# The first norm of a two-layer trunk, fed tile by tile of x, with three pairs of weight column tiles in flight

## The chip, the cores and the metric

The kernel runs as one program on one NeuronCore of one Trainium2 chip. The metric is the device time in microseconds of one execution; lower is better. Before the change it is 1466.57 us (median of 3 runs, 1466.33 to 1467.88).

The engines are named as the profile names them: PE is TensorE (matmuls; PEld its weight loads), DVE is VectorE, ACT is ScalarE, POOL is GpSimd, and SP is SyncE, whose queue issues nearly all loads here. Each engine works through its own queue in order; an instruction whose input is missing holds up everything behind it on that engine.

## The reference, cut to what matters

Two layers of a diffusion backbone over 384 tokens of width 1024: 128 context tokens and 256 latent ones, each group with its own conditioning vector. Each layer is FFN, mixer, FFN, and each of the three is modulated by nine vectors per layer:

```
mod = silu(cond) @ w_mod[l] + b_mod[l]                 # (1024) @ (1024, 9216), one cond per group
sh1, sc1, g1, sh2, sc2, g2, sh3, sc3, g3 = split(mod, 9)
x = x + 0.5*g1 * swiglu(modulate(rmsnorm(x, norm_g[l,0]), sh1, sc1), w1, w3, w2)
x = x + g2 * mixer(modulate(rmsnorm(x, norm_g[l,1]), sh2, sc2))
x = x + 0.5*g3 * swiglu(modulate(rmsnorm(x, norm_g[l,2]), sh3, sc3), ...)
rmsnorm(x, g)  = x * rsqrt(mean(x*x) + eps) * g ;  modulate(x, sh, sc) = x*(1+sc) + sh
swiglu(x, ...) = (silu(x @ w1) * (x @ w3)) @ w2        # 1024 -> 2816 -> 1024, all float32
```

Before the first matmul of the first FFN can run, the kernel needs sh1 and sc1 of layer 0 (8 MB of w_mod), x (1.5 MB) and the first weights.

## The kernel before, in words

Everything is transposed: x lies in SBUF as 8 K tiles of 128 rows (features) by 384 columns (tokens). All weights are 128x128 tiles, packed on the host in the order in which the program reads them, 16 tiles to a 1 MB chunk (156 chunks). Every float32 product is made of three float32r matmuls: each weight and each activation is split into a high part (a rounded copy, `hi`) and a low part (the rest, `lo`), and `mm3` (line 436) issues hi*hi, hi*lo, lo*hi. So one weight tile is three matmuls of 384 or 386 columns, and one chunk is 48. `w_split` (391) makes `hi` of half a chunk (8 tiles) by a copy on ACT or DVE, and `w_lo` (410) makes `lo` on DVE; when both halves are split, the chunk's buffer is free and `w_load` (381) asks SP for another one. There are 3 chunk buffers (`rawp`, line 261).

In the first FFN the norm is not applied to x ahead of the matmul. `prep` (522) scales a tile of x by A = norm_g*(1+sc1), a column per token group, and appends the shift sh1 as two extra columns (386 columns); the factor rsqrt(mean(x*x)) is a number per token and is multiplied in when PSUM is read (`up_evac`, 649). `rstd_chain` (546) gets that factor from the sum of squares that `prep` collects, by one matmul with a matrix of 1/1024. `normed_all` (560) meanwhile makes the fully normed x on the idle DVE; from some column tile on the FFN uses it instead.

`ffn` (602) loops over 22 column tiles f; each has a w1 and a w3 column of 8 K tiles, 16 weight tiles, 48 matmuls. For f = 0 the last K tile comes last for both; otherwise the whole w1 column is made and then the w3 column. Each f has a pair of PSUM banks (tag `sc`, two pairs).

The start is written out by hand. The 8 MB of w_mod for sc1 (k = 1) and then sh1 (k = 0) come in eight 1 MB tiles, four per vector: rows of K, 1024 columns. For each, 8 matmuls with silu(cond) as weights (32 columns wide, four of them side by side in the array) add to one PSUM tile; the result is two rows of 1024, which two transposes turn into columns. Only after all four tiles of sc1 are added does A exist, and `prep` runs for all eight tiles of x; only after all four of sh1 do the two shift columns exist. The loads stand on SP's queue in this order: four tiles for sc1, the eight tiles of x, four for sh1, three weight chunks, and then what is needed later (c as rows, two tiles of w_mod for DVE, tables).

All other modulation vectors (128 tiles of 0.5 MB) are made on DVE by `mod_one` (476), when it has nothing else to do; the program's own rough clock (`Clock`, `Sched`) decides while the program is written where such side work is put between the matmuls. It orders the instructions and nothing else.

Of the kernel before, what the change touches and what calls it, by code (L numbers as in the profile page):

```python
# [19 lines left out]
P = 128  # L20
NP_, NS = 128, 256
T = NP_ + NS
TB = T + 2
# [7 lines left out]
N_SLAB = 79  # L31
# [16 lines left out]
class Event:  # L48
    """Something that a chain of instructions has still to emit, with the tiles that it leaves."""
# [5 lines left out]
class Banks:  # L55
    """PSUM tiles of one tag: how many may be in use at a time, and when the free ones fell free."""
# [5 lines left out]
class Idle:  # L62
    """Ready when an engine has nothing else queued."""
# [19 lines left out]
class Clock:  # L83
    """Rough times of the engines while the program is written: they order the emission and nothing else."""
# [34 lines left out]
class Sched:  # L119
    """Emits the stages of side chains between pieces of the matmul stream, each when its inputs should be there."""  # L120
# [81 lines left out]
class Eng:  # L202
    """An engine's instructions, timed by the clock as they are written."""
# [50 lines left out]
def emit(tc, D, order):  # L254
    nc = tc.nc
    ctx = ExitStack()
    with ctx:
# [3 lines left out]
        rawp = pool("raw", 3)  # L261
# [60 lines left out]
        def copy(out, in_, scale=None):  # L322
            """out = in_ (times a column), on the engine that should be done with it first."""
            k = {} if scale is None else {"scale": scale}
            r = max(clock.at(in_)[0], clock.at(out)[0])
            ta = max(clock.free["ACT"], r) + S_.cost("activation", out, [in_], k)
            td = max(clock.free["DVE"], r) + V.cost("tensor_copy", out, [in_] if scale is None else [in_, scale], k)
            if td + ON_ACT < ta:
                if scale is None:
                    V.tensor_copy(out, in_)  # L330
                else:
                    V.tensor_scalar(out, in_, scale, None, ALU.mult)
            else:
                act(out, in_, AF.Copy, **k)

# [36 lines left out]
        class WS:  # L372
            raw, hi, lo, rest = {}, {}, {}, {}
            asked, due = set(), []
            loaded = split = n = 0
# [5 lines left out]
        def w_load():  # L381
            c = WS.loaded
# [93 lines left out]
        def mod_one():  # L476
            """Generator: one modulation tile, a condition per stage."""
# [17 lines left out]
        mod_on = Event()  # L495

        def mod_all():
# [16 lines left out]
        class XS:  # L514
            hi, lo, ev, sq, A, sh = [], [], [], None, None, None
# [6 lines left out]
        def prep(d, with_sh=True):  # L522
            """Generator: scaled x as two float32r parts, and the sum of squares."""
            q = sl()
            hi = XS.hi[d] = sl(F32R, TB)
            lo = XS.lo[d] = sl(F32R, TB)
            act(q, x[d], AF.Square)
# [4 lines left out]
            yield hi, q  # L532
            if XS.sq is None:
                XS.sq = q
            else:
                V.tensor_tensor(XS.sq, XS.sq, q, ALU.add)
# [4 lines left out]
            sched.fire(XS.ev[d], hi, lo, XS.sq)  # L541
# [4 lines left out]
        def rstd_chain():  # L546
# [11 lines left out]
            sched.add(gen(RS.t, RS.ev, XS.ev))  # L558
# [43 lines left out]
        def ffn(l, n, nxt):  # L602
# [6 lines left out]
            for f in range(FF):  # L609
# [24 lines left out]
                sched.add(up_evac(ps, hs[f]))  # L634
# [14 lines left out]
        def up_evac(ps, h):  # L649
            yield ps  # L650
            bc = small.tile([P, 2, 2], F32, tag="bc2", name=nm("bc"))
            V.tensor_copy(bc, ps[:, :, T:TB])
            t, u = sl(), sl()
            V.tensor_tensor(t, ps[:, 0, :T], RS.t, ALU.mult)
            V.tensor_tensor(u, ps[:, 1, :T], RS.t, ALU.mult)
            free(scb, ps, u)
# [57 lines left out]
        def qk_norm(t, bc, gate, gs):  # L714
            """Generator: leaves the normed rows in t, then returns the two parts of the rotated ones."""
# [107 lines left out]
        def transposed(src, n):  # L823
            """w (128 queries, n*128 keys) -> SBUF (keys, n, queries)."""
# [22 lines left out]
        def proj_pass(tiles, key, done, low):  # L847
            """Projection tiles in order; the first two share a K order that leaves the last tile of x late."""
# [32 lines left out]
        def out_pass(key, gm, nxt, ready, free_at, early, wide):  # L881
            """Output projection. The K tiles in `early` come first: x takes their part while the others are computed."""
# [8 lines left out]
            def slot(t, ps):  # L891
                """A bank that has nothing to do: kept while there are units to come."""
# [351 lines left out]
        def wm_load(i):  # L1244
            t = rawp.tile([P, 2, 1024], F32, tag="raw", name=nm("wm0"))
            nc.sync.dma_start(t, D["wm0"][i])
            landed(t, 1 << 20, sched.now())
            return t

        def mixer_consts():  # L1250
            yield RS.ev, el, pp
            # differential lambda, negated
# [5 lines left out]
            # -8 * softplus(-lam) on (128, 2 directions, 4 tiles); log1p by its series in z / (2 + z)  # L1258
# [24 lines left out]
        wm0 = [wm_load(i) for i in range(3)]  # L1283
        for k in (1, 0):
            ps = mmt()
            for i in range(4):
                w = wm0.pop(0)
                for s in range(2):
                    for g in range(4):
                        TE.matmul(ps[32 * g:32 * g + 32, 0:256], lhsT=scT[:, 2 * i + s, :],  # L1290
                                  rhs=w[:, s, 256 * g:256 * (g + 1)], start=i + s == 0, stop=i + s == 4)
                j = (4 if k == 0 else 0) + i + 3
                if j < 8:
                    if j == 4:
                        for d in range(KD):
                            nc.sync.dma_start(x[d], D["xT"][d])  # L1296
                    wm0.append(wm_load(j))
                else:
                    w_load()
                    if j == 10:  # L1300
                        nc.sync.dma_start(cbc, D["c_rows"].partition_broadcast(P))
                        landed(cbc, 1 << 20)
                        mod_load(nc.sync)
                        mod_load(nc.sync)
                        nc.sync.dma_start(cst, D["cst"])
                        nc.sync.dma_start(el, D["e_lam"].partition_broadcast(P))
                        landed(el, 1 << 19)
            mrow = sl()
            V.tensor_copy(mrow[:, 0:256], ps[:, 0:256])
            free(mmb, ps, mrow)  # L1310
            pt = mst()
            for b in range(2):
                TE.transpose(pt[:, b * P:(b + 1) * P], mrow[:, b * P:(b + 1) * P], ident)
            M[0, k] = cpool.tile([P, 8, 2], F32, name=f"M0_{k}")
            pv = pt[:, 0:256].rearrange("p (c g r) -> p g c r", c=2, g=4)
            V.tensor_copy(M[0, k].rearrange("p (g c) j -> p g c j", g=4), pv[:, :, :, 0:2])
            free(msb, pt, M[0, k])
            mod_finish(0, k)
            mod_done.add((0, k))
            if k == 1:  # L1320
                prep_begin(0, 0)
                for d in range(KD):
                    for _ in prep(d, False):
                        pass
        sched.add(mod_all(), 2)
        sched.fire(mod_on)
        RS.ev = Event()
        XS.sh = M[0, 0]
        w_split()
        for d in range(KD):  # L1330
            act(XS.hi[d][:, T:TB], XS.sh[:, d, :], AF.Copy)
        w_lo(0, WS.rest[0])
        for d in range(KD):
            V.tensor_tensor(XS.lo[d][:, T:TB], XS.sh[:, d, :], r32(XS.hi[d][:, T:TB]), ALU.subtract)
# [6 lines left out]
        ffn(0, 0, (0, 1))  # L1341
# [8 lines left out]
# order of the 64 rows of a q or k head on the partitions: the two rows of a rotary pair side by side  # L1350
# [136 lines left out]
```

## Time and profile before

| | |
|---|---|
| median of 3 runs | 1466.57 us |
| span of the profiled execution | 1464.2 us |
| PE busy | 1436.7 us, 98% |
| DVE busy | 1115.4 us, 76% |
| ACT busy | 659.8 us, 45% |
| DMA, mean over the span | 171 GB/s, 250.67 MB |

The profiled execution's own time is its span of 1464.2 us and what lies around the span; the median of the runs is 2.4 us above the span. In the 40 slices of the page the PE row is `4999999999999999999999999999999999999998`: of the whole program only the first slice (36.6 us) is not full. The row that names the engine of the chain that ended last says PE 95%, DMA 2%, DVE 2%.

How to read it: an engine's share is a mean over stages. What a change at the start is worth must be read from the start itself: when the first column tiles are done, and which of loads, DVE and PE is the last to be ready for them.

### The profile page before, as it was taken

To read this page: it belongs to the slowest core of one execution; us is meant where nothing else is said; L and a number is where in the kernel's file an instruction comes from. 1 tells how busy PE (TensorE), PEld (TensorE's weight loads), DVE (VectorE), ACT (ScalarE), POOL (GpSimd) and SP (SyncE) were. 2 spreads that over 40 slices of the span, in tenths; PEclk is the share of its full clock that TensorE was granted. 3 is DMA by queue.
4 is the path that set the end of the run, shared out by engine and by line. 5 is a ranking of instruction groups with operands and counts; after the bars stand their busy time and mean duration, and the time that the engine had idled before them with its cause. 6 is when DMAs were issued, how large, how long until landed. Compare 5 with 4: busy or idle time off the path is not lost.

```text
span 1464.2 us, 21823 instructions
## 1 busy us (share of the span) xinstructions
PE 1436.7 (98%) x8354; PEld 1398.4 (96%) x8354; DVE 1115.4 (76%) x2103; ACT 659.8 (45%) x1193; POOL 103.8 (7%) x214
## 2 busy tenths in 40 slices
PE   4999999999999999999999999999999999999998
PEld 1999999998889999999999999999998899999998
DVE  3899999969998998999979997444698795444332
ACT  3643333348875633333345333333477664333321
POOL 0001111110220011111100110000100000000000
PEclk9999999999999999999999999999999999999999
DMA  9557767652322366766744766333331233333430
GB/s 361 216 185 257 246 245 257 235 173 101 120 99 97 140 230 236 254 243 231 254 177 153 251 243 196 135 119 130 117 107 51 77 120 115 133 126 116 146 135 22
DMA packets 49560, 250.67 MB, mean 171 GB/s; under 512 B 6464, under 2 KB 10960, under 8 KB 28336
## 3 DMA queue, kind: packets, MB, share of 16 engines
q1 hardware_dynamic: 29664, 180.05, 34.0%
q0 software_dynamic: 19792, 69.23, 14.2%
q8 instruction: 66, 1.08, 0.3%
q14 instruction: 38, 0.31, 0.1%
HBM read 244.53 MB, written 2.36 MB: 169 GB/s over the span
## 4 chain that ended last, share of the span: by engine, by line
PE 95%; DMA 2%; DVE 2%; ACT 1%; issue 0%; SPq 0%; DVEq 0%; ACTq 0%
PE sc L214 54%; PE mm L214 36%; PE ms L214 5%; DVE s L214 1%; DMA wm<-in_wm 1%; DMA s<-in_xT 1%; DMA raw<-in_wst 0%; DVE lo L214 0%; ACT s L214 0%; DMA s<-s 0%; ACT hi L214 0%; ACT L317 0%; SPq L737 0%; SPq L1296 0%; DVEq L1434 0%
## 5 line engine op out<-in xcount | busy, mean ns | idle before, releaser
L214 PE MATMUL sc<-s,hi 128*128 128x384 f32 (+1 forms) x2816 | 726.3, 339 | 2.3 <-ACT s L214 1.4
L214 ACT ACTIVATE hi<-raw 128x1024 fp32r<-128x1024 f32 x298 | 315.7, 1060 | 541.7 <-PE sc L214 307.4
L214 DVE TENSOR_TENSOR lo<-raw,hi 128x1024 fp32r<-128x1024 f32 x312 | 381.3, 1223 | 231.2 <-ACT hi L214 230.0
L214 PE MATMUL mm<-s,hi 128*128 128x384 f32 (+1 forms) x2072 | 545.8, 344 | 2.3 <-DVE s L214 2.3
L214 PEld LDWEIGHTS sc<-s,hi 128*128 128x128 f32 x2816 | 512.6, 188 | 5.0 <-ACT s L214 1.8
L214 PE MATMUL sc<-s,lo 128*128 128x384 f32 (+1 forms) x1408 | 475.4, 338 | 0.0
L214 PEld LDWEIGHTS mm<-s,hi 128*128 128x128 f32 x2072 | 372.9, 188 | 12.4 <-issue 3.0
L214 PE MATMUL mm<-s,lo 128*128 128x384 f32 (+1 forms) x1036 | 349.1, 337 | 0.0
L214 DVE CUSTOM_DVE_ANT_0 junk<-wm,cbc 128x1024 bf16<-128x1024 f32 x256 | 312.6, 1221 | 11.0 <-DMA wm<-in_wmt 8.3
L214 PEld LDWEIGHTS sc<-s,lo 128*128 128x128 f32 x1408 | 265.0, 188 | 0.0
L214 PEld LDWEIGHTS mm<-s,lo 128*128 128x128 f32 x1036 | 194.7, 188 | 0.0
L214 ACT ACTIVATE s<-s 128x384 f32<-128x384 f32 (+3 forms) x215 | 108.0, 507 | 171.9 <-DVE s L214 157.0
L214 DVE TENSOR_TENSOR s<-s,s 128x384 fp32r<-128x384 f32 (+6 forms) x214 | 112.0, 528 | 20.0 <-ACT s L214 18.9
L214 POOL DMA_DIRECT2D wm<-in_wmt x126 | 66.6, 528 | 695.1 <-DVE M L214 674.2
L214 DVE SCALAR_TENSOR_TENSOR s<-s,M,s 128x128 fp32r<-128x128 f32 (+3 forms) x256 | 92.4, 416 | 3.8 <-ACT s L214 3.7
L214 ACT ACTIVATE s<-s,M 128x256 fp32r<-128x256 f32 (+1 forms) x167 | 66.3, 446 | 11.0 <-DVE s L214 8.1
L214 DVE SCALAR_TENSOR_TENSOR s<-mm,M,s 128x128 f32<-128x128 f32 x104 | 38.5, 412 | 32.2 <-PE mm L214 32.2
L214 DVE TENSOR_TENSOR s<-sc,s 128x384 f32<-128x384 f32 x106 | 56.8, 551 | 0.0
L214 PE MATMUL sc<-s,s 128*128 128x384 f32 (+2 forms) x208 | 49.0, 373 | 0.7 <-ACT s L214 0.7
L214 ACT ACTIVATE s<-ms 128x384 f32<-128x384 f32 (+3 forms) x80 | 31.8, 423 | 29.8 <-PE ms L214 29.5
L214 PEld LDWEIGHTS sc<-s,s 128*128 128x128 f32 x208 | 34.1, 189 | 7.0 <-ACT s L214 1.3
L214 ACT ACTIVATE s<-sc,sm 128x385 f32<-128x385 f32 (+3 forms) x72 | 35.9, 511 | 0.0
(107 smaller groups left out, 635.1 us busy)
## 6 DMA issues: line engine op xcount, KB each, us to landing
raw<-in_wst SPq DMA_DIRECT2D x156, 1024.0 KB, 5.0
wm<-in_wmt POOLq DMA_DIRECT2D x126, 512.0 KB, 3.8
wm<-in_wm SPq DMA_DIRECT2D x8, 1024.0 KB, 7.6
s<-s SPq DMA_DIRECT2D x36, 64.0 KB, 2.4
s<-in_xT SPq DMA_DIRECT2D x8, 192.0 KB, 7.4
out_y<-s SPq DMA_DIRECT2D x8, 192.0 KB, 1.9
cbc<-in_c_rows SPq DMA_DIRECT2D x1, 1024.0 KB, 8.4
wm<-in_wmt SPq DMA_DIRECT2D x2, 512.0 KB, 9.7
```

The lines of the kernel that those rows point to most:

```text
L214: r = fn(*a, **k)
```

## The change

- The eight w_mod tiles are cut the other way. `wm0[d]` holds columns d*128 to d*128+127 of sc1 and of sh1 with all of their 1024 rows, 8 KB per partition in one row. One 1 MB load gives A and sh1 of x's tile d alone. Per tile `first_mod` issues 8 matmuls as before, copies the PSUM rows to SBUF on DVE, and turns them into columns by two matmuls with a 128x2 selector (`sel`), which also adds up the four parts; two DVE instructions read PSUM and leave A and sh1 of this tile, and `prep` of this tile follows.
- The eight loads use six buffers: `cbc` (0, 4), the two halves of `modp` (1, 5), and chunk buffers (2, 3, 6, 7), of which there are now 4 (before 3). The slab of 384-column tiles has 74 (before 79).
- On SP's queue the tiles of x and the first weight chunks stand between them.
- The squares of x are summed by a chain of their own (`first_sq`), as x lands.
- The first FFN starts with `lead=3`: three column tiles f = 0, 1, 2 share the K loop. For each K tile of x all six columns (w1, w3 of three f) get their three matmuls, 18 in all; f = 2 uses the two `mm` banks.
- DVE's modulation tiles, their silu and the constants of the mixer wait for `calm`, which is fired at f = 5; the first 48 modulation tiles then no longer stop during the mixer.
- `up_evac` copies the two shift columns with two instructions, since the two banks may be apart.
- While the first tiles are loaded, `w_next` splits weights ahead only once their chunk has landed.

The diff, cut to its core:

```diff
-N_SLAB = 79
+N_SLAB = 74
...
-        rawp = pool("raw", 3)
+        rawp = pool("raw", 4)
...
             while WS.split <= min(g + 3, 2 * N_CHUNK - 1):
+                if WS.split > g and (WS.split // 2 not in WS.raw and WS.first or WS.split // 2 in WS.raw
+                                     and clock.at(WS.raw[WS.split // 2])[0] > sched.now() + 0.5):
+                    break
                 w_split()
...
         def mod_all():
-            yield cbc, RS.ev
+            yield cbc, calm
             act(cbc, cbc, AF.Silu)
             while mod_at[0] < len(mod_todo):
-                yield mod_on
+                if mod_at[0] >= 48:
+                    yield mod_on
                 yield from mod_one()
...
-            for f in range(FF):
+            if lead:
+                up = []
...
+                for k in range(8):
+                    sched.wait(XS.ev[k])
+                    for f in range(lead):
+                        for m in range(2):
+                            mm3(up[f][m][:, :TB], ("w1" if m == 0 else "w3", l, n, k, f), XS.hi[k], XS.lo[k], k == 0, k == 7)
+                        if k == 7:
+                            sched.wait(RS.ev)
+                            hs.append([None, None, Event()])
+                            sched.add(up_evac(*up[f], hs[f]))
+            for f in range(lead, FF):
+                if f == lead + 2:
+                    sched.fire(calm)
...
+        def first_mod(d):
+            w = m0.pop(d)
+            yield tuple(w) + (msb,)
+            ps = mst()
+            for i in range(2):
+                for g in range(4):
+                    j = 2 * g + i
+                    TE.matmul(ps[32 * g:32 * g + 32, 0:256], lhsT=scT[:, j, :], rhs=w[j], start=i == 0, stop=i == 1)
+            if d == 1:
+                c_load()
+            if d + 4 < KD:
+                m_load(d + 4)
...
+            r = sl(w=256)
+            yield ps
+            V.tensor_copy(r, ps[:, 0:256])
+            yield r
+            for i in range(2):
+                TE.matmul(ps[:, 256 + 2 * i:258 + 2 * i], lhsT=r[:, i * P:(i + 1) * P], rhs=sel, start=True, stop=True)
+            yield ps, x[d]
+            V.scalar_tensor_tensor(M[0, 1][:, d, :], ps[:, 256:258], b_one[:, d:d + 1], ...)
+            V.tensor_scalar(M[0, 0][:, d, :], ps[:, 258:260], pp[:, o:o + 1], None, ALU.add)
+            yield M[0, 0]
+            yield from prep(d, squares=False)
...
+        m_load(0)
+        x_load(0)
+        c_load()
+        x_load(1)
+        m_load(1)
+        x_load(2, 3)
+        m_load(2)
+        x_load(4)
+        c_load()
+        x_load(5)
+        m_load(3)
+        x_load(6, 7)
...
-        ffn(0, 0, (0, 1))
+        ffn(0, 0, (0, 1), lead=3)
```

How it moves instructions. The first place is the start of SP's queue. Before, from the first w_mod load on (`wm` and `in_wm` are the w_mod tiles, `s_94` to `s_101` the tiles of x, `raw` the weight chunks; the other six tiles of x and the last w_mod tiles follow):

```order
L1246 DMA wm_121<-in_wm 128x2048
L1246 DMA wm_123<-in_wm 128x2048
L1246 DMA wm_125<-in_wm 128x2048
L1246 DMA wm_136<-in_wm 128x2048
L1296 DMA s_94<-in_xT 128x384
L1296 DMA s_95<-in_xT 128x384
```

The same place now:

```order
L1330 DMA cbc<-in_wm 128x2048
L1347 DMA s_94<-in_xT 128x384
L395 DMA raw_129<-in_wst 128x2048
L1347 DMA s_95<-in_xT 128x384
L1336 DMA wm_132<-in_wm 128x1024
L1336 DMA wm_133<-in_wm 128x1024
L1347 DMA s_96<-in_xT 128x384
L1347 DMA s_97<-in_xT 128x384
L1341 DMA wm_138<-in_wm 128x2048
L1347 DMA s_98<-in_xT 128x384
L395 DMA raw_141<-in_wst 128x2048
```

The first tile of x and the first weight chunk now stand directly behind the first w_mod tile; two weight chunks stand ahead of the fourth w_mod tile, and a third one ahead of the sixth.

The second place is PE's queue around the last w_mod tile. Before, that tile is `wm_265`, `ms_306` are the transposes of sh1, and `sc_341` is the PSUM of the FFN's first column tile:

```order
L214 MATMUL mm_256<-wm_174,scT 32x256 x8
L214 MATMUL mm_256<-wm_265,scT 32x256 x8
L214 MATMUL ms_306<-ident,s_304 128x128 x2
L214 MATMUL sc_341<-s_186,hi_312 128x386
L214 MATMUL sc_341<-s_187,hi_312 128x386
L214 MATMUL sc_341<-s_186,lo_322 128x386
```

Now that tile is `wm_332` (tile 7 of x), `s_400` and `s_401` are the two parts of x's tile 4, `s_469` and `s_470` those of tile 5:

```order
L214 MATMUL mm_160<-s_400,hi_290 128x386
L214 MATMUL mm_160<-s_401,hi_290 128x386
L214 MATMUL mm_160<-s_400,lo_305 128x386
L214 MATMUL ms_494<-wm_332,scT 32x256 x8
L214 MATMUL sc_157<-s_469,hi_290 128x386
L214 MATMUL sc_157<-s_470,hi_290 128x386
L214 MATMUL sc_157<-s_469,lo_305 128x386
```

Before, no FFN matmul stands ahead of the last w_mod tile; now the 90 of x's tiles 0 to 4 do, and the 54 of tiles 5 to 7 stand behind it. From the fourth column tile (f = 3) on, PE's queue is the same as before, row by row, to the end of the program.

The third place is DVE's queue around the low part of x's last tile. Before, that tile's low part is `s_249`, and the first weights' low part is `lo_322`:

```order
L214 SCALAR_TENSOR_TENSOR s_249<-s_101,M_1_181,s_248 128x128
L214 SCALAR_TENSOR_TENSOR s_249<-s_101,M_1_181,s_248 128x256
L214 COPY s_304<-mm_256 128x256
L214 COPY M_0_309<-ms_306 128x16
L214 TENSOR_TENSOR M_0_309<-M_0_309,pp 128x16
L214 TENSOR_TENSOR lo_322<-raw_275,hi_312 128x1024
```

Now the low part of the last tile is `s_557`, `M_1_122` and `M_0_121` are its A and sh1, `hi_546` to `lo_574` are the weights of f = 3, and `s_543` is the low part of the fully normed x (tile 3):

```order
L214 SCALAR_TENSOR_TENSOR M_1_122<-ms_494,b_one,pp 128x2
L214 TENSOR_SCALAR M_0_121<-ms_494,pp 128x2
L214 CAST hi_546<-raw_371 128x1024
L214 CAST hi_548<-raw_371 128x1024
L214 TENSOR_TENSOR lo_564<-raw_371,hi_546 128x1024
L214 SCALAR_TENSOR_TENSOR s_543<-s_530,M_0_121,s_542 128x128
L214 SCALAR_TENSOR_TENSOR s_543<-s_530,M_0_121,s_542 128x256
L214 TENSOR_TENSOR lo_574<-raw_371,hi_548 128x1024
L214 SCALAR_TENSOR_TENSOR s_557<-s_101,M_1_122,s_556 128x128
L214 SCALAR_TENSOR_TENSOR s_557<-s_101,M_1_122,s_556 128x256
```

Before, all low parts of x stand ahead of the first weight split; now eight weight halves and four tiles of the normed x are split ahead of the last tile's low part.

## Rows read from the trace of the kernel before

**Rows 1.** Stages: from:to length, busy us (count) PE PEld DVE ACT POOL, PEclk, DMA, GB/s
```profile
0.00:36.30 36.30, 16.53 (x133) 5.53 (x133) 12.39 (x39) 12.97 (x36) 2.19 (x10) 0.95 0.94 360
36.30:63.80 27.50, 27.48 (x146) 26.88 (x147) 24.54 (x83) 19.41 (x31) 0.00 (x0) 0.95 0.56 215
63.80:1460.50 1396.70, 1392.69 (x8077) 1366.02 (x8075) 1077.75 (x1982) 627.44 (x1128) 101.65 (x204) 1.00 0.47 166
1460.50:1464.20 3.70, 0.00 (x0) 0.00 (x0) 0.74 (x2) 0.00 (x0) 0.00 (x0) 0.78 0.15 53
```

**Rows 2.** Chain that ended last, first 60 us: start us, us, what
```profile
1.20 5.24 DMA wm<-in_wm
...
16.92 7.94 DMA wm<-in_wm
...
26.90 6.96 DMA raw<-in_wst
```

**Rows 3.** PE timeline: start us, us, instruction, count, idle before and its releaser
```profile
6.57 1.93 PE L214 MATMUL mm<-wm,scT 128*32 128x256 f32 x16 [6.57 <-DMA wm<-in_wm]
9.61 1.93 PE L214 MATMUL mm<-wm,scT 128*32 128x256 f32 x16 [1.10 <-DMA wm<-in_wm]
12.15 1.93 PE L214 MATMUL mm<-wm,scT 128*32 128x256 f32 x16 [0.61 <-DMA wm<-in_wm]
...
31.42 1.07 PE L214 MATMUL mm<-wm,scT 128*32 128x256 f32 x16 [2.21 <-DMA wm<-in_wm]
33.04 0.69 PE L214 MATMUL ms<-ident,s 128*128 128x128 f32 x2 [0.55 <-DVE s L214]
35.08 0.69 PE L214 MATMUL sc<-s,hi 128*128 128x386 f32 x1 [1.36 <-ACT s L214]
36.32 0.69 PE L214 MATMUL sc<-s,hi 128*128 128x386 f32 x1 [0.55 <-DVE s L214]
...
39.84 0.52 PE L214 MATMUL sc<-s,hi 128*128 128x386 f32 x2
...
40.37 0.51 PE L214 MATMUL sc<-s,hi 128*128 128x386 f32 x2
```

**Rows 4.** Stages of the start, columns as in rows 1
```profile
13.00:31.00 18.00, 9.37 (x78) 2.87 (x70) 9.69 (x27) 9.05 (x24) 0.00 (x0) 1.00 1.03 406
33.00:36.00 3.00, 1.38 (x3) 0.58 (x3) 1.38 (x3) 2.12 (x10) 0.00 (x0) 0.50 0.94 352
36.00:38.00 2.00, 1.68 (x5) 1.38 (x5) 2.00 (x12) 1.98 (x3) 0.00 (x0) 0.50 1.03 434
39.50:40.00 0.50, 0.50 (x4) 0.50 (x3) 0.50 (x2) 0.50 (x1) 0.00 (x0) 1.00 0.99 410
```

**Rows 5.** DVE timeline, columns as in rows 3
```profile
17.89 0.42 DVE L214 COPY s<-mm 128x256 f32<-128x256 f32 x1 [16.44 <-PE mm L214]
19.15 0.17 DVE L214 COPY M<-ms 128x16 f32<-128x16 f32 x1 [0.84 <-PE ms L214]
...
20.21 0.88 DVE L214 SCALAR_TENSOR_TENSOR s<-s,M,s 128x128 fp32r<-128x128 f32 x2 [0.47 <-ACT s L214]
21.03 0.56 DVE L214 TENSOR_TENSOR s<-s,s 128x384 f32<-128x384 f32 x1
21.50 0.74 DVE L214 SCALAR_TENSOR_TENSOR s<-s,M,s 128x128 fp32r<-128x128 f32 x2
22.16 0.55 DVE L214 TENSOR_TENSOR s<-s,s 128x384 f32<-128x384 f32 x1
...
36.81 0.68 DVE L214 CAST hi<-raw 128x1024 fp32r<-128x1024 f32 x1
37.42 3.49 DVE L214 TENSOR_TENSOR lo<-raw,hi 128x1024 fp32r<-128x1024 f32 x3
...
72.41 0.16 DVE L214 COPY bc<-sc 128x4 f32<-128x4 f32 x1 [0.74 <-PE sc L214]
```

**Rows 6.** PE's waits from 63.8 us on: who for whom, us in total, times, longest
```profile
PE mm L214 <- DVE s L214: 2.3, 2, 2.0
```

More of the change, by code (lines that the diff above doesn't have):

```diff
@@ L374, in emit @@
             asked, due = set(), []
-            loaded = split = n = 0
+            loaded = split = n = held = 0
+            first = True
         def landed(t, nbytes, after=0.0):
@@ L381, in w_load, with c_load @@
         def w_load():
+            if WS.first:
+                WS.held += 1
+            else:
+                c_load()
+        def c_load():
             c = WS.loaded
@@ L531, in prep @@
                 copy(hi[:, T:TB], XS.sh[:, d, :])
-            yield hi, q
-            if XS.sq is None:
+            yield (hi, q) if squares else hi
+            if not squares:
+                pass
+            elif XS.sq is None:
                 XS.sq = q
@@ L557, in gen @@
                 sched.fire(ev, out)
-            sched.add(gen(RS.t, RS.ev, XS.ev))
+            sched.add(gen(RS.t, RS.ev, [XS.sq_ev] if XS.sq_ev else XS.ev))
+            XS.sq_ev = None
         def normed_all(low):
@@ L599, in epilogue, with ffn @@
             sched.add(gen())
-        def ffn(l, n, nxt):
+        def ffn(l, n, nxt, lead=0):
             sched.fire(mod_on)
@@ L633, in ffn @@
                 hs.append([None, None, Event()])
-                sched.add(up_evac(ps, hs[f]))
+                sched.add(up_evac(ps[:, 0, :], ps[:, 1, :], scb, hs[f]))
             xn = None
@@ L1241, in odd_mixer @@
             out_pass("o_out", (1, 5), nxt, ready, [ready[k][2] for k in range(8)], list(range(O_EARLY)), WIDE_O)
[L1244 to L1248, printed above, removed]
         def mixer_consts():
-            yield RS.ev, el, pp
+            yield calm, el, pp
             V.tensor_scalar(gsub, par("subln"), 1.0 - LAM_INIT, None, ALU.mult)
@@ L1282, in emit @@
         act(scT[:, :, 0:2], craw, AF.Silu)
[L1283 to L1297, printed above, removed]
-                else:
[L1299 to L1324, printed above, removed]
@@ new lines, in emit, with m_load @@
+        for k in range(2):
+            M[0, k] = cpool.tile([P, 8, 2], F32, name=f"M0_{k}")
+            mod_done.add((0, k))
+        sel = cpool.tile([P, 2], F32, name="sel")
+        V.tensor_reduce(sel, ident.rearrange("p (g r) -> p r g", g=4)[:, 0:2, :], AX.X, ALU.add)
+        b_one = cpool.tile([P, 8], F32, name="b_one")
+        V.tensor_scalar(b_one, pp[:, PPC["b_mod"][0] + 8:PPC["b_mod"][0] + 16], 1.0, None, ALU.add)
+        prep_begin(0, 0)
+        m0 = {}
+        def m_load(d):
+            if d % 4 == 0:
+                m0[d] = [cbc.rearrange("p a b -> p (a b)")[:, j * 256:(j + 1) * 256] for j in range(8)]
+                nc.sync.dma_start(cbc.rearrange("p a b -> p (a b)"), D["wm0"][d])
+                landed(cbc, 1 << 20, sched.now())
+            elif d % 4 == 1:
+                two = [modp.tile([P, 1024], F32, tag="wm", name=nm("wm")) for _ in range(2)]
+                m0[d] = [t[:, j * 256:(j + 1) * 256] for t in two for j in range(4)]
+                for i, t in enumerate(two):
+                    nc.sync.dma_start(t, D["wm0"][d][:, i * 1024:(i + 1) * 1024])
+                    landed(t, 1 << 19, sched.now())
+            else:
+                t = rawp.tile([P, 2048], F32, tag="raw", name=nm("wm0"))
+                m0[d] = [t[:, j * 256:(j + 1) * 256] for j in range(8)]
+                nc.sync.dma_start(t, D["wm0"][d])
+                landed(t, 1 << 20, sched.now())
+            sched.add(first_mod(d))
@@ new lines, in x_load, with rest_load @@
+        def x_load(*ds):
+            for d in ds:
+                nc.sync.dma_start(x[d], D["xT"][d])
+                landed(x[d], 196608)
+        def rest_load():
+            nc.sync.dma_start(cbc, D["c_rows"].partition_broadcast(P))
+            landed(cbc, 1 << 20)
+            mod_load(nc.sync)
+            mod_load(nc.sync)
+            nc.sync.dma_start(cst, D["cst"])
+            nc.sync.dma_start(el, D["e_lam"].partition_broadcast(P))
+            landed(el, 1 << 19)
+        def first_mod(d):
[10 more added lines that the diff above has]
+                m_load(d + 4)
+            if d == 4:
+                WS.first = False
+                for _ in range(WS.held):
+                    c_load()
+            if d == KD - 1:
+                rest_load()
+            r = sl(w=256)
[5 more added lines that the diff above has]
+            yield ps, x[d]
+            o = PPC["norm_g"][0] + d
+            V.scalar_tensor_tensor(M[0, 1][:, d, :], ps[:, 256:258], b_one[:, d:d + 1], pp[:, o:o + 1].to_broadcast([P, 2]),
+                                   ALU.add, ALU.mult)
+            o = PPC["b_mod"][0] + d
+            V.tensor_scalar(M[0, 0][:, d, :], ps[:, 258:260], pp[:, o:o + 1], None, ALU.add)
+            free(msb, ps, M[0, 0])
+            yield M[0, 0]
+            yield from prep(d, squares=False)
@@ new lines, in first_sq @@
+        def first_sq(ev):
+            for d in range(KD):
+                yield x[d]
+                q = sl()
+                act(q, x[d], AF.Square)
+                yield q
+                if d == 0:
+                    XS.sq = q
+                else:
+                    V.tensor_tensor(XS.sq, XS.sq, q, ALU.add)
+            sched.fire(ev, XS.sq)
+        m_load(0)
+        x_load(0)
+        c_load()
+        x_load(1)
[3 more added lines that the diff above has]
+        x_load(4)
@@ L1325, in emit @@
+        c_load()
+        x_load(5)
+        m_load(3)
+        x_load(6, 7)
+        XS.sq_ev = Event()
+        sched.add(first_sq(XS.sq_ev))
         sched.add(mod_all(), 2)
-        sched.fire(mod_on)
         RS.ev = Event()
[L1328 to L1334, printed above, removed]
```

35 lines of the change are left out of this document (23 added, 12 removed).

## The prediction

> **What bounds the kernel now.** I read the stages first. From 63.8 us to 1460.5 us PE is busy 1392.69 of 1396.70 us [rows 1]: there is nothing to gain there, and the change leaves PE's queue in that stretch as it was. In the first 36.3 us PE is busy 16.53 us, and with w_mod and transposes only; the DMA engines are busy 0.94 of that time. The chain that ended last names the loads: a w_mod load from 1.20 us, another from 16.92, a weight chunk from 26.90 [rows 2]. So the first stage is bound by loads that come one after the other while PE has no FFN work. PE's timeline says when that ends: the first FFN matmul is at 35.08, the second at 36.32, and from 39.84 on a weight tile's three matmuls take 0.53 us (39.84 to 40.37), 0.177 us each [rows 3].
>
> The mark for the whole argument is the time at which PE starts f = 3, since all that follows is the same queue. Before: the three matmuls from 39.84 are the fourth weight tile, so tile 49 starts at 39.84 + 45 x 0.533 = 63.8. DVE confirms it: it waits for the end of f = 3 until 72.41 [rows 5], and 63.8 + 48 x 0.177 = 72.3. The question is when the changed kernel has done the same 144 matmuls.
>
> **The change part by part.** There are four queues to follow, and the last one to be ready sets the mark.
>
> *Loads.* SP's order now has d0, x0, chunk 0 (2.3 MB), then x1, d1 (3.5), x2, x3, d2 (5.0), x4, chunk 1, x5, d3 (7.5), x6, x7, d4 (8.9), chunk 2 (10.0), d5, d6, d7 (13.1 MB). From 13 to 31 us the queue moved 406 GB/s at a busy share of 1.03 [rows 4]; I use 0.41 MB per us. The first MB lands at 1.20 + 5.24 = 6.4 [rows 2]; PE's waits put the second and third at 9.6 and 12.1 [rows 3], 0.6 later than 0.41 gives. So chunk 0 lands at 6.4 + 1.25/0.41 + 0.6 = 10.1, and d7 at 6.4 + 12.05/0.41 + 0.6 = 36.4. Rows of 8 KB, or of 4 KB for d1 and d5, I cost at nothing: the before's w_mod loads already saturate the engines. Behind d7 PE has its 8 small matmuls (1.07) and 54 FFN matmuls (9.6), so the loads alone would allow 36.4 + 1.1 + 9.6 + 0.3 = 47.4.
>
> The Trainium skill ("DMA: Bandwidth & Descriptors", section Specifications) gives a limit of about 358 GB/s per core for HBM; the 406 GB/s of this trace is above that, and by the page's figure d7 would land at 40.7 and this bound would be 51.7.
>
> *PE.* Its FFN work can start when the first weights are split: chunk 0 at 10.1, a DVE copy of half of it (0.68 [rows 5]) behind the low part of x0, so about 12.5. Behind it stand 144 x 0.177 = 25.6 us, seven w_mod tiles at 1.07 (31.42 [rows 3]) = 7.5, and the mean square's matmul and seven selector pairs. Neither shows in this form; two transposes took 0.69 at half rate [rows 3], so a selector pair is between 0.05 and 0.69, taken as 0.3, and the mean square as 0.7, as much as the two transposes: 2.8 together. Sum 35.9 at full rate.
>
> The rate is not full at first. The column PEclk reads 1.00 up to 31 us, yet the same 16 matmuls take 1.93 us at 6.57 and 1.07 at 31.42 [rows 3]; the durations say 1.2 GHz for most of the mod phase. The clock is granted at 0.50 again from 33 to 38 us and full by 39.5 [rows 4], about 4 us after the FFN matmuls begin at 35.08. I take the same 4 us here, which costs 2. PE without waits: 12.5 + 35.9 + 2 = 50.4.
>
> *DVE.* From the first weight split (10.1 at the earliest, 10.9 behind x0's low part) to the low part of x's last tile it has: 8 lows of weights at 3.49/3 = 1.16 (9.3), 6 copies at 0.68 (4.1), 7 sums of squares at 0.47, 21.03 to 21.50 (3.3), 15 pairs of the two token groups at 0.66, 21.50 to 22.16 (9.9; 7 for the low parts of x, 8 for the normed x), 7 copies out of PSUM at 0.42 (2.9), 14 small ones for A and sh1 at 0.2 (2.8), shift columns and one copied tile (1.2) [all rows 5]: 33.5 us, to 44.4. It also waits: for each tile it must get the w_mod sum from PE and the high part from ACT. The before shows one such pair: 0.84 for PE and 0.47 for ACT [rows 5]. In most tiles other work covers one of the two, so I take 0.84 x 7 = 5.9; bounds are 0 and 7 x 1.31 = 9.2. So the last low part is there at 50.3, and 17 matmuls (3.0) follow: 53.3.
>
> *Both together.* PE and DVE wait for each other in turn, so the mark is later than either. Walking both orders with these durations, PE waits for DVE at the first low weights (0.6), at the low parts of tile 1 (0.4), tile 4 (1.8) and tile 7 (0.9), 3.7 in all. I add these to PE's 50.4: 54.1. From DVE's side I had 53.3. I take 54.0, which is 9.8 us before the old mark.
>
> *The rest.* ACT was busy 12.97 us in the first stage [rows 1] with much the same work, and has room. The evacuation of f = 0 must be read before f = 3 can write its pair of banks; DVE comes to it about 2.9 us after the last low part, while PE needs 3.2 us for the last tile, so up to 0.5 us may show. Weight chunk 3 lands at 39 and chunk 4 at 42, ahead of use. The modulation tiles start later: the one that ends the second norm's scale is done, counted in split weight halves, at half 42 of the 44 of the up phase, and was at 38; a half is 8 x 0.533 = 4.3 us, so 8.5 us of slack are left and I cost it at nothing. After 63.8 PE waited on DVE for 2.3 us in two places [rows 6]; four or five slab buffers less and one copy more per f could add a little: -1 to +3 us, taken as 0.
>
> The sum: the span of 1464.2 less 9.8 is 1454.4. The median of the runs is 2.4 above the profiled span; with that, 1456.8 us.
>
> **The rivals.**
>
> - *The loads are the only bound.* DVE's waits are covered and the clock rises at once; the mark is 47.4 to 51, and the time 1450.2 to 1453.8. For it: the load share of 0.94 now. Against: PE's own sum is 50.4 already. 0.13.
> - *Handovers cost more.* Every tile pays both waits (9.2), or the clock rises ten us later (+5): the mark is 57 to 59.5, the time 1459.8 to 1462.3. For it: seven chains of PE, DVE, PE, DVE, ACT, DVE in place of two. Against: there is other work in each queue. 0.17.
> - *PE stays at half rate (the other side).* Every 1 us at half rate costs 0.5. At half rate throughout the stretch, PE needs 12.5 + 2 x 35.9 = 84.3, and the time is 1466.6 + 20.5 = 1487. It is slower than before from the point where the rate stays at half for some 20 us beyond my 4. For it: in the mod phase PE was busy about half of the time (9.37 of 18 us [rows 4]) and stayed at half rate for 20 us. Against: at half rate a tile of x is 18 x 0.354 + 1.93 = 8.3 us of PE work for 4 us of loads, so PE would have no gaps, as after 35.08. 0.04. The Trainium skill ("TensorE: Matmul & The Clock Gate", section What's actually happening) says that the slow clock is the default and activity lifts it; the durations above agree, and by that rule this rival is open while PE is fed by loads.
> - *Given back later.* The modulation tiles, late by four halves, make PE wait at the end of the up phase or in the mixer; if a forced row of them costs ten us, no change is left: 1464 to 1467. 0.06.
>
> **How the numbers follow.** My forecast (mark 52 to 57, 1454 to 1460) has 0.60; with the others that is 1. Within 0.2% (2.9 us) of 1466.57 a measurement of this kernel can't tell it from no change. Faster: forecast, first and second rival and a little, 0.91. Same: 0.05, the last rival. Slower: 0.04, the third. The range of 1451 to 1462 holds the forecast and most of the first two rivals.
>
> **What would show it.** In the changed profile DVE's wait for the end of f = 3 should end near 54.0 + 8.6 = 62.6 instead of 72.4. d7's small matmuls should be past 36.4. PE's waits before the mark should be on DVE (tiles 4 and 7), not on a load, and DVE should be nearly full from 11 to 53 us. 128x386 matmuls should show 0.34 us from about 17 us on. The stage behind the mark should be as long as now, 1400.4 us to the end. I am wrong if the mark is past 60 or before 50, or if that stage is over 3 us longer.

## The result, and the profile after

The changed kernel took 1456.93 us (median of 4 runs, 1456.46 to 1458.8); the kernel before, run beside it, took 1466.45 (4 runs, 1464.9 to 1467.88). The ratio is 0.994 with an interval of 0.9928 to 0.9953. The forecast was 1456.8 us. The profiled execution has a span of 1454.7 us (1464.2 before).

PE's timeline of the changed kernel up to the mark (start us, us, instruction, count, idle before and its releaser; the first w_mod buffer carries the name `cbc` here):

```profile
6.21 1.94 PE L214 MATMUL ms<-cbc,scT 128*32 128x256 f32 x16 [6.21 <-DMA cbc<-in_wm]
...
12.13 0.98 PE L214 MATMUL sc<-s,hi 128*128 128x386 f32 x2 [2.43 <-DVE hi L214]
13.29 0.69 PE L214 MATMUL sc<-s,lo 128*128 128x386 f32 x1 [0.18 <-DVE lo L214]
...
14.88 1.87 PE L214 MATMUL ms<-wm,scT 128*32 128x256 f32 x16
16.68 0.62 PE L214 MATMUL sc<-s,hi 128*128 128x386 f32 x2
17.14 0.34 PE L214 MATMUL sc<-s,lo 128*128 128x386 f32 x1
...
17.85 0.51 PE L214 MATMUL ms<-sel,s 128*128 128x2 f32 x4
18.22 0.60 PE L214 MATMUL mm<-s,hi 128*128 128x386 f32 x2
...
19.45 1.07 PE L214 MATMUL ms<-wm,scT 128*32 128x256 f32 x16
20.45 0.63 PE L214 MATMUL sc<-s,hi 128*128 128x386 f32 x2
...
37.41 0.44 PE L214 MATMUL sc<-s,hi 128*128 128x386 f32 x1 [1.22 <-DVE s L214]
...
42.66 1.07 PE L214 MATMUL ms<-wm,scT 128*32 128x256 f32 x16
...
51.16 0.45 PE L214 MATMUL sc<-s,hi 128*128 128x386 f32 x1 [0.21 <-DVE s L214]
...
54.26 0.52 PE L214 MATMUL sc<-s,hi 128*128 128x386 f32 x2
```

The first FFN matmul starts at 12.13; before, it was at 35.08 [rows 3]. The mark, f = 3's first matmul, is the last row: 54.26 in place of 63.8. From 12.13 on PE waits three times, always on DVE: 0.18, 1.22 (tile 4) and 0.21 (tile 7). No load holds it any more. The last w_mod tile, whose small matmuls are those at 42.66 (8 in the program, 16 in the trace), landed at 36.9 (issued at 26.1, landed 10.8 us later), well ahead of its place in PE's queue.

The chain that ended last says the same. Of its first 15 us in the changed kernel (start us, us, what):

```profile
1.20 4.87 DMA cbc<-in_wm
...
12.02 1.24 DVE lo L214
13.29 1.66 PE sc L214 x4
```

One load stands in it, the first. Before, the chain named w_mod loads and a weight chunk up to 33.9 us [rows 2]. Behind that it is now PE, with a few DVE pieces.

The stages of the changed kernel (from:to, length, busy us and count of PE, PEld, DVE, ACT, POOL, granted clock, DMA share, GB/s), six us each up to 54:

```profile
12.00:18.00 6.00, 5.69 (x31) 3.56 (x31) 3.87 (x6) 1.27 (x3) 0.00 (x0) 1.00 1.05 422
18.00:24.00 6.00, 6.00 (x48) 5.17 (x47) 4.37 (x15) 2.88 (x8) 0.00 (x0) 1.00 1.02 411
24.00:30.00 6.00, 6.00 (x46) 4.47 (x49) 4.84 (x12) 2.80 (x5) 0.00 (x0) 1.00 1.02 416
30.00:36.00 6.00, 6.00 (x55) 4.51 (x55) 5.24 (x16) 3.60 (x9) 0.00 (x0) 1.00 1.02 421
36.00:42.00 6.00, 4.78 (x40) 3.87 (x39) 4.98 (x14) 0.89 (x3) 0.00 (x0) 1.00 0.62 233
42.00:48.00 6.00, 6.00 (x46) 5.17 (x47) 5.51 (x17) 3.39 (x10) 0.00 (x0) 1.00 1.01 410
48.00:54.00 6.00, 5.79 (x33) 5.47 (x32) 6.00 (x16) 2.51 (x4) 0.00 (x0) 1.00 1.01 320
```

PE is busy 40.26 of these 42 us; in the first 36.3 us before it was busy 16.53 [rows 1]. Up to 36 us, where the queue is full, the loads are as fast as they were (DMA share 1.02 to 1.05, 411 to 422 GB/s): the same transfers, with PE's work now beside them. DVE has 34.8 of 42 us. The clock column reads 1.00 throughout, but the durations don't: the 16 small matmuls take 1.94 us at 6.21, 1.87 at 14.88 and 1.07 at 19.45, and a 128x386 matmul takes 0.69 at 13.29 and 0.34 at 17.14. The pair at 16.68, directly behind a w_mod tile, already takes 0.62, as the pair in the same place does at 20.45 (0.63). So PE ran at its lower level (1.2 GHz) until about 16.7 us.

The stage behind the mark is 1454.7 - 54.26 = 1400.4 us, as before (1464.2 - 63.8). The whole gain was made ahead of the mark.

### The profile page after: what moved, and what is told of

Its sections match the earlier page's. It is cut to its first block, busy times and chain, and to the rows that moved or that the text cites. A ratio compares the mean times of both kernels' runs of the same rounds, so it can differ in the third digit from the quotient of the medians.

```text
span 1454.7 us, 21900 instructions
## 1 busy us (share of the span) xinstructions
PE 1436.7 (99%) x8382; PEld 1400.9 (96%) x8382; DVE 1127.8 (78%) x2153; ACT 649.7 (45%) x1180; POOL 104.1 (7%) x214
## 4 chain that ended last, share of the span: by engine, by line
PE 97%; DVE 2%; ACT 1%; issue 0%; DMA 0%; DVEq 0%; SPq 0%; ACTq 0%
PE sc L214 53%; PE mm L214 37%; PE ms L214 6%; DVE s L214 1%; DVE lo L214 0%; DMA cbc<-in_wm 0%; ACT s L214 0%; ACT hi L214 0%; DVE hi L214 0%; ACT L317 0%; DVE M L214 0%; DVEq L1521 0%; SPq L339 0%; DVE sm L214 0%; DVEq L214 0%
## 5 line engine op out<-in xcount | busy, mean ns | idle before, releaser
L214 PE MATMUL sc<-s,hi 128*128 128x384 f32 (+1 forms) x2784 | 718.5, 339 | 4.3 <-DVE hi L214 2.4
L214 PE MATMUL mm<-s,hi 128*128 128x384 f32 (+1 forms) x2104 | 554.5, 345 | 2.2 <-DVE s L214 2.2
L214 ACT ACTIVATE hi<-raw 128x1024 fp32r<-128x1024 f32 x288 | 305.4, 1060 | 532.8 <-PE sc L214 303.8
L214 PEld LDWEIGHTS sc<-s,hi 128*128 128x128 f32 x2784 | 506.4, 188 | 9.0 <-DVE s L214 3.1
L214 PE MATMUL sc<-s,lo 128*128 128x384 f32 (+1 forms) x1392 | 470.6, 338 | 0.2 <-DVE lo L214 0.2
L214 PEld LDWEIGHTS mm<-s,hi 128*128 128x128 f32 x2104 | 379.0, 188 | 12.8 <-issue 3.4
L214 PE MATMUL mm<-s,lo 128*128 128x384 f32 (+1 forms) x1052 | 355.0, 337 | 0.0
L214 PEld LDWEIGHTS mm<-s,lo 128*128 128x128 f32 x1052 | 197.8, 188 | 0.0
L214 DVE SCALAR_TENSOR_TENSOR s<-s,M,s 128x256 fp32r<-128x256 f32 (+3 forms) x256 | 92.1, 410 | 4.1 <-ACT s L214 4.0
## 6 DMA issues: line engine op xcount, KB each, us to landing
wm<-in_wm SPq DMA_DIRECT2D x4, 1024.0 KB, 10.8
wm<-in_wm SPq DMA_DIRECT2D x4, 512.0 KB, 10.8
```

The costliest lines, as they stand in the source:

```text
L214: r = fn(*a, **k)
```

## The experiments

Each was run beside the kernel before (1466.55, 1466.46 or 1465.61 us). The mark is read from PE's timeline: it is the start of the 145th FFN matmul, the first of f = 3. It can't be had as the span less 1400.4, since the stage behind the mark is not equally long in all runs (the end of the next section has its lengths). e2, e3, e4, e5, e6, e7, e10 and e12 were timed once each.

**How many column tiles run beside the loads.** e1 changes one number, as below; e2 puts lead=2 there:

```diff
-        ffn(0, 0, (0, 1), lead=3)
+        ffn(0, 0, (0, 1), lead=1)
```

> The mark is the start of f = 3 on PE: 63.8 us before the change, 54.3 with it. Theory (the gain is FFN matmuls laid beside the loads): with one column tile in the K loop instead of three only 48 matmuls can lie there; the last w_mod tile lands near 36.5, its chain takes about 5, and 6 + 96 matmuls follow: mark 59 to 61, time 1462 to 1464. Rival (the gain is the new queue order and the K-wise w_mod; the number of column tiles does not matter): mark 54, time 1457.

> Two column tiles in the K loop. Theory: PE was nearly without gaps from 12 us on with three, and 96 of 144 matmuls fit as well: after the last tile's chain at 41 to 42 us come 12 + 48 matmuls, 10.6 us, so loads would allow 52 and PE's own sum 53 to 54: mark 53 to 55, span within 1 us of 1454.7. Rival (each column tile less costs a third of the gain of 9.6 us): mark 57.5.

e1 took 1470.83 us (8 runs, 1470.04 to 1471.88; ratio to before 1.003, 1.0019 to 1.0041), span 1469.6, mark 71.1. e2 took 1460.37, span 1458.6, mark 61.4: above the 53 to 55 expected and above the rival's 57.5. The first column tile less costs 7.2 us of the mark and the second 9.7 (3.9 and 11.0 us of the span), so the overlap is where the gain is. e2 loses a part to the clock too: its granted clock is 0.72 from 36 to 42 us. But e1's mark is 10 us later than I expected, and the run is slower than the kernel before. Its stages say why (columns as above):

```profile
24.00:30.00 6.00, 4.53 (x26) 2.85 (x26) 5.33 (x11) 4.28 (x8) 0.00 (x0) 1.00 1.01 417
30.00:36.00 6.00, 5.44 (x38) 3.62 (x42) 3.36 (x15) 2.12 (x5) 0.00 (x0) 0.72 1.02 414
36.00:42.00 6.00, 3.64 (x26) 2.89 (x22) 6.00 (x17) 3.81 (x10) 0.00 (x0) 0.71 0.30 124
42.00:48.00 6.00, 5.45 (x39) 2.82 (x39) 3.75 (x16) 2.48 (x8) 0.00 (x0) 0.50 0.50 176
```

With one column tile, PE has gaps (4.53 busy of 6, later 3.64), and the granted clock falls to 0.72 and then 0.50. At these levels 6 x (0.28 + 0.29 + 0.50) = 6.4 us of PE's full rate are missing from 30 to 48 us. That is an upper bound for these stages, since PE was idle in part of them. Ahead of 30 us the column says nothing: it reads 1.00, but a pair of 386-column matmuls takes 0.85 us, where 0.52 is the full rate (54.26 in the changed kernel):

```profile
26.17 0.85 PE L214 MATMUL sc<-s,hi 128*128 128x386 f32 x2
```

**Whether the gaps themselves cost.** e12 keeps lead=1 and fills the gaps with 56 matmuls into a bank that nobody reads:

```diff
+                    if k == 0:
+                        fill = mmt()
+                    for _ in range(8 if k < 7 else 0):
+                        TE.matmul(fill[:, :TB], lhsT=XS.hi[k][:, 0:P], rhs=XS.hi[k], start=True, stop=True)
```

> One column tile in the K loop as in the run that came out slower than before (mark 69), but with eight matmuls of 386 columns behind each of the first seven K tiles that write a PSUM bank nobody reads. Theory (that run lost 8 us to half rate, since PE had gaps): PE stays at full rate, and the loads with the last tile's chain set the mark: 59 to 62, span 1459.4 to 1462.4, faster by adding work. Rival (the clock is not it; the DVE chain per tile is): 69 or later, span 1469 to 1472.

1465.32 us, span 1463.6, mark 66.4: 4.7 us earlier than e1, with more work, and 6.0 us less span. The mark lies between the theory's 59 to 62 and the rival's 69, so the theory promised too much. The same stages of e12, and a w_mod tile of its PE timeline:

```profile
24.00:30.00 6.00, 4.79 (x36) 3.48 (x35) 5.55 (x14) 3.06 (x5) 0.00 (x0) 1.00 1.01 413
30.00:36.00 6.00, 5.85 (x53) 3.88 (x51) 4.92 (x19) 4.76 (x12) 0.00 (x0) 1.00 1.02 420
36.00:42.00 6.00, 4.56 (x40) 3.64 (x40) 6.00 (x19) 2.07 (x6) 0.00 (x0) 1.00 0.32 116
42.00:48.00 6.00, 6.00 (x47) 5.42 (x47) 4.90 (x21) 3.76 (x12) 0.00 (x0) 1.00 0.93 375
```
```profile
26.64 1.07 PE L214 MATMUL ms<-wm,scT 128*32 128x256 f32 x16
```

The clock stays at 1.00 in all four, and here the durations agree (1.07 us). PE comes to its last w_mod tile at 41.98, in e1 at 45.38. Up to there DVE's queue differs from e1's by two swaps only, so these 3.4 us are what the fallen clock cost e1. Behind it the program, which orders side work by its own clock, put DVE's work differently, and the other 1.3 us of the mark can be due to that. e12 is still 12.2 us behind the changed kernel (66.4 against 54.3): the 96 matmuls of f = 1 and 2, which run from 49.5 to 66.4, stand behind the loads instead of beside them.

**Whether loads bound the new start.** e5 moves the first two weight chunks behind x's last two loads. e7 puts a copy of 1.57 MB in DRAM ahead of the load of w_mod tile 6:

```diff
+            if d == 2:
+                nc.sync.dma_start(D["y"], D["xT"])
```

and e5:

```diff
-        c_load()
...
-        c_load()
...
+        c_load()
+        c_load()
```

> A copy of x (1.57 MB) into the output's place in DRAM, which is overwritten later, stands on the queue ahead of the last two w_mod tiles: about 4 us more of loads. Theory (loads are not the bound: the last w_mod tile lands near 36.5 and PE comes to it at 42.7): mark 54.3 to 55. Rival (loads set the mark): mark 58.

> Only the queue order is undone in part: the two weight chunks stand behind the first four w_mod tiles and all tiles of x. Theory: the first chunk lands 4.5 MB later, near 21 us instead of 10, FFN matmuls start at 22 to 23, four w_mod tiles are already done, and 144 matmuls, four w_mod tiles and some half rate follow: mark 56.5 to 59. Rival (the loads up to the last w_mod tile set the mark, and their sum is the same): mark 54.3.

e7 took 1456.56 us, span 1454.8, mark 54.0: the changed kernel's time. The last w_mod tile lands at 40.8 instead of 36.9, and PE comes to it at 42.4. The stage in which the changed kernel's DMA engines were 0.62 busy is full here:

```profile
36.00:42.00 6.00, 4.86 (x40) 4.15 (x41) 4.84 (x16) 0.90 (x3) 0.00 (x0) 1.00 1.02 422
```

So the queue had room, and loads are not the bound. e5 took 1464.07, span 1462.3, mark 62.8: later than the 56.5 to 59 expected. PE's wait in e5 (engine, what, for whom: total us, times, longest) is

```profile
PE sc L214 <- ACT hi L214: 9.7, 1, 9.7
```

and PE's rows behind it, from 22.33 us on, are at the lower level: a w_mod tile at 24.21 takes 1.93 us, as at 6.21 in the changed kernel. PE was at the lower level ahead of the wait too, and reaches the upper one only at about 29.7 us. That costs about half of 7 us, 3.5 us, more than the "some half rate" that I had allowed for. Early weights are needed for the gain.

**Less PE work.** e6 leaves out half of w_mod's rows (one of two matmuls for each column group), so that PE has about 4 us less in the same stretch.

```diff
-            for i in range(2):
+            for i in range(1):
```

> Half of the small matmuls on the w_mod tiles are left out (half of the 1024 rows do not enter sc1 and sh1 of layer 0's first norm), so PE has 8 x 0.54 = 4.3 us less to do up to the mark; loads and DVE's work are as they were. Theory (PE is the nearest bound, DVE close behind): mark 50.5 to 52. Rival A (DVE is the bound): 53.5 to 54.3. Rival B (PE alone): 50.

1457.53 us, span 1455.8: no gain. The mark is 57.1, later than the theory and both rivals had it. Two views of e6, a stage and PE's waits:

```profile
30.00:36.00 6.00, 5.72 (x24) 4.43 (x24) 2.09 (x9) 2.32 (x6) 0.00 (x0) 0.50 1.01 411
```
```profile
PE sc L214 <- DVE s L214: 3.4, 4, 1.4
...
PE ms L214 <- DVE s L214: 1.1, 2, 0.5
```

PE's gaps came back (these two waits are 1.8 and 0.5 us in the changed kernel), and with them the clock of 0.50: 5.72 x 0.5 = 2.9 us of PE's rate. Together that is 5.1 us, more than the 4.3 that the work left out was to give. The mark is 2.8 us later, so a part is not accounted for. The edit also changed the order of DVE's queue from 11 us on, and no run filled e6's gaps as e12 did e1's: this account is argued, not shown.

**A warm start, and the later norm.** e4 (repeated as e11) lets PE multiply the identity, 9 times ahead of the first w_mod tile and 5 times behind its selector pair. e3 holds the normed copies of x back until the lead loop is over; e8 is both. e9 is e4 with the norm released at K tile 4; e10 releases it at tile 5.

```diff
+        def busy(n):
+            w = mst()
+            for _ in range(n):
+                TE.matmul(w[:, 0:P], lhsT=ident, rhs=ident, start=True, stop=True)
+            free(msb, w, w)
+        busy(9)
...
+            if d == 0:
+                busy(5)
```
For the norm, `gate` is `(led,)`; the event fires behind the lead loop in e3 and e8, and as below in e9 (k == 5 in e10, which also moves the pause for other work one f ahead, to lead + 1):

```diff
-                yield rs_ev, DVE_IDLE
+                yield (rs_ev, DVE_IDLE) + gate
...
+                    if k == 4:
+                        sched.fire(led)
```

> Matmuls of a constant keep PE busy from 3 us to the first w_mod tile and between its selector pair and the first FFN matmul; nothing else changes. Theory: the first six FFN matmuls and the second w_mod tile, at half rate until about 16.6 us, run at full rate: 1 + 0.8 us less, of which a wait for the first low weights takes some back: mark 52.4 to 53.5. Rival (the late start at 12.1 us and DVE set it): mark 54.3.

> The kernel with PE kept busy from 3 us once more, timed. Theory: 0.9 us below the changed kernel as in its profile: 1455.8 to 1456.3. Rival (that was chance): 1456.9.

e4: 1455.66 us, span 1453.9, mark 53.4. e11: 1455.77 (5 runs, 1455.67 to 1455.87), ratio to before 0.9927 (0.9914 to 0.9939), mark 53.7. That is the gain of about one us that was expected, but it does not lie where the expectation put it. PE in e4:

```profile
6.53 1.07 PE L214 MATMUL ms<-cbc,scT 128*32 128x256 f32 x16 [0.27 <-DMA cbc<-in_wm]
...
11.18 0.59 PE L214 MATMUL sc<-s,hi 128*128 128x386 f32 x2 [1.21 <-DVE hi L214]
...
13.93 1.94 PE L214 MATMUL ms<-wm,scT 128*32 128x256 f32 x16
15.79 0.62 PE L214 MATMUL sc<-s,hi 128*128 128x386 f32 x2
```

The first w_mod tile runs at the upper level (1.07 us in place of 1.94), so the FFN starts 0.95 us earlier, at 11.18. Behind that start the level falls again: the second w_mod tile takes 1.94 us, and the full rate is back at 15.79. The FFN matmuls were to gain and did not; the first w_mod tile did.

> The fully normed x of the first FFN (8 tiles on DVE and ACT) starts only behind the three column tiles. Theory: PE waits on DVE 1.2 us at tile 4 and 0.2 at tile 7 because normed tiles stand ahead of the low parts; both go: mark 52.9 to 53.2, span 1453.4 or so. Rival A (DVE sets the mark by its sum of work; 4 normed tiles with 8 pairs of 0.66 leave it): mark 49 to 50. Rival B (PE is the only bound): mark 54.3, no change.

> Both edits that should take waits away together: PE kept busy from 3 us on, and the normed x behind the three column tiles. Theory: 1.4 and 0.8 to 1.9 us add up: mark 51 to 52.3, span 1451.5 to 1452.8, time 1453.7 to 1455. Rival (the second wait comes back on DVE once the first is gone): mark 53, time 1455.7.

> As the run held back to tile 4, but to tile 5; the last early modulation tile then is at weight half 71 of the program, behind the FFN's 66 and early in the mixer. Theory: the mixer's scale is needed only at its end, so three halves more cost nothing or up to 3 us; mark 52, span 1452 to 1455. Rival (any tile pushed into the mixer costs as in the run with half 89): span 1460 or more.

e3 took 1471.71 us, e8 1471.42 (1469.16 to 1473.85; ratio to before 1.0033, 1.0021 to 1.0045), e10 1466.06. Their marks are 53.8, 52.6 and 53.9: earlier than the changed kernel's 54.26, but none as early as the 52.9 to 53.2, 51 to 52.3 and 52 that were expected. In e3 PE's waits on the parts of x in the lead loop fall from 1.4 to 0.6 us. What the three gained was lost far behind, in the mixer: their stages behind the mark are 1416.1, 1416.8 and 1410.4 us. The same 60 us in the changed kernel and in e10:

```profile
440.00:500.00 60.00, 59.59 (x336) 58.86 (x335) 57.89 (x143) 38.07 (x76) 0.00 (x0) 1.00 0.35 120
```
```profile
440.00:500.00 60.00, 54.85 (x287) 53.36 (x288) 55.30 (x133) 34.14 (x67) 1.70 (x3) 0.94 0.31 106
```

and PE's waits in that stretch of e3:

```profile
PE mm L214 <- ACT s L214: 6.3, 2, 3.2
PE mm L214 <- DVE s L214: 2.6, 3, 1.1
```

The order of the instructions names the cause, and e9 beside e10 bears it out. The modulation tile that ends the third norm's scale is done at weight half 68 in the changed kernel (63 before), at 71 in e10 and at 89 in e3 and e8. The modulation tiles left over then fall into the mixer, where DVE and ACT have work for PE. At 68 this costs nothing; three halves more cost e10 some ten us. How the late tiles hold up the mixer's own instructions was not followed through the trace.

> PE kept busy from 3 us, and the normed x of the first FFN held back only to K tile 4 instead of to the end of the three column tiles; the last early modulation tile stays at weight half 68 as in the changed kernel (it was at 89 where the normed x was held back to the end). Theory (that run lost its 14 us to late modulation tiles in the mixer, not to the start): mark 52 to 52.8, the stage behind it 1400.4 as before, span 1452.4 to 1453.2, time 1454.2 to 1455. Rival (holding the normed x back costs by itself, through the later switch to it): span above 1455.

e9 keeps that tile at half 68. It took 1451.84 us (4 runs: 1456.14, 1451.79, 1451.65, 1451.89), ratio to before 0.99 (0.9884 to 0.9915), whose interval lies below that of the changed kernel: the best version here. Only the run of 1456.14 has a trace. Its mark is 54.8, later than the changed kernel's and than the 52 to 52.8 expected, and in it PE was at the lower level longer than in e4:

```profile
12.00:18.00 6.00, 5.59 (x26) 3.41 (x27) 3.79 (x7) 1.36 (x3) 0.00 (x0) 0.50 1.04 418
```

The wait at tile 4, the longest of the changed kernel, is 0.6 us there. The trace has a second such stretch, in the mixer. Behind a wait of 2.00 us PE is at the lower level until about 322.4 us, which costs some 1.6 us; the changed kernel has nearly the same wait in the same place and keeps the upper level. First e9, then the changed kernel:

```profile
318.71 0.69 PE L214 MATMUL mm<-s,hi 128*128 128x386 f32 x2 [2.00 <-DVE s L214]
319.20 0.53 PE L214 MATMUL mm<-s,lo 128*128 128x386 f32 x1
```
```profile
318.40 0.59 PE L214 MATMUL mm<-s,hi 128*128 128x386 f32 x2 [1.96 <-DVE s L214]
318.83 0.34 PE L214 MATMUL mm<-s,lo 128*128 128x386 f32 x1
```

Why the other three runs are 4.3 us shorter stays open. The late mark (2 us or more) and this stretch would make up most of it, but no trace shows that the three were without them. Their mean granted clock was 1.000 against 0.996, which says little: the changed kernel's is 1.000 too, with a start at the lower level.

## Why the prediction was right

The forecast was 1456.8 us, the measurement 1456.93; the mark 54.0, measured 54.26. The mechanism is the one forecast: FFN matmuls beside the loads, PE and DVE close together as the bound, an unchanged stage behind the mark. That the mark came out within 0.3 us is in part luck, as PE's terms show. Step by step:

- *Loads.* Shown. They were to allow a mark of 47.4. The last w_mod tile landed at 36.9 (forecast 36.4), and PE reached it at 42.66, about 6 us later. e7 shows that 1.57 MB more cost nothing. The rival that loads alone are the bound (0.13) falls. The Trainium skill ("DMA: Bandwidth & Descriptors", section Specifications) has about 358 GB/s per core; the changed kernel's rows again show 411 to 422, so here the measurement decides.
- *PE.* Start 12.5, measured 12.13. Half rate was to cost 2.0; it lasted from 12.13 to about 16.7, less the wait of 0.18, and so cost 2.2. The waits were 3.7, measured 1.6 (0.18 + 1.22 + 0.21; the one at tile 1 was covered). The work was 35.9: 54.26 - 12.13 - 2.2 - 1.6 leaves 38.3. So two terms were off by 2 us each and cancelled by luck: the waits too large, the work too small. Most of the missing work can be seen in PE's rows: a selector group goes from 17.85 to 18.22, and the seven of them take 0.36 to 0.55 us, 2.9 in all in place of 2.1; and the first 386-column pair behind a group of another shape shows 0.60 us where a pair in a row shows 0.52, about twelve times, 1.0 in all.
- *DVE.* The last low part was to be there at 50.3. DVE's row for it in the changed kernel (start us, us, instruction) starts at that time, and ends at 51.0:

```profile
50.29 0.74 DVE L214 SCALAR_TENSOR_TENSOR s<-s,M,s 128x128 fp32r<-128x128 f32 x2
...
62.95 0.23 DVE L214 COPY bc<-sc 128x2 f32<-128x2 f32 x2
```

  PE goes on at 51.16 and reaches the mark 3.1 us later (forecast 3.0). The second row, the end of f = 3, was forecast for 62.6. "Nearly full" was too strong for DVE: it is busy 34.8 of 42 us, much as the forecast's own 33.5 of work and 5.9 of waits say. PE had waited only 0.21 us for this low part, so both queues came to that point nearly together, as forecast. e4, e3 and e8 agree: an earlier start of PE moves the mark by 0.9 us, less work on DVE in the loop by 0.5, and both together by 1.7.
- *The rest.* The stage behind the mark was to be unchanged: 1400.4 both times. The modulation tiles that come later cost nothing, but I had looked at the second norm's tile (half 42 of 44) only. The third norm's, at 68, is the one with its edge near: e10 falls over it at 71. The rival "given back later" (0.06) is real three halves further on.
- *Half rate.* The rival at 0.04 was priced as an all-or-nothing case. The runs show a rate that depends on how PE is fed: e1 loses by it, e12 gains by adding work, and e6, which got nothing for less work, fits this. "At half rate PE would have no gaps" was the right reason here, and it holds for three column tiles and not for one. Of the 16.9 us by which e1's mark is behind the changed kernel's, e12 takes back 4.7, of which 3.4 are shown to be the clock's. The three column tiles therefore do two things, they fill the load time and they hold PE's clock up; the prediction had priced the first only.

Not settled: e9's spread, and the stage behind the mark. Where no modulation tile came late it is 1400.4 to 1400.8 us before, in the changed kernel and in e4, e7 and e11, but 1399.5 in e5 and e9, 1398.7 in e6, 1398.5 in e1, 1397.2 in e2 and 1397.1 in e12. PE's waits behind the mark are the same in the changed kernel, e2 and e12; the difference grows slowly over some 900 us, and its cause was not looked for.

## What to carry to other kernels

Where an unchanged queue follows a reworked start, find the one instruction at which the two join, and forecast its time from each engine's queue apart; the rest of the span needs no model. Price a gap in PE's stream as more than its length: the rows behind it may run at the lower clock, so filler work can be worth its time (e12), and removed work was worth nothing in e6. Before side work is pushed back, look up its last due place for every consumer, not for the next one.

## What the hardware showed beside it

In these traces the granted-clock column reads 1.00 from the first row until its first change, while the durations tell of the lower level (1.94 us against 1.07 for the same 16 matmuls, both at 1.00); durations decide. PE was at the lower level on both sides of a wait of 9.7 us (e5). The level fell in stretches where PE waited tile after tile (e1, and e6 with no wait over 0.61 us between 16 and 30 us), and in e1's places filler matmuls held it (e12). Nearly the same wait in the mixer let it fall in e9 (2.00 us) and not in the changed kernel (1.96 us), so the length of one wait did not decide it. Where the queue was full, the loads held 406 to 422 GB/s on one core, whether PE worked beside them (411 to 422) or was busy half of the time (406 [rows 4]).
